# Splitting the two parts of a weight tile in TensorE's queue: high parts first, low parts second

## The chip, the cores and the metric

The kernel runs on one core of a Trainium2 chip. Its metric is the device time in microseconds (us) of one execution of the whole program. Before the change three runs took 1864.05, 1870.47 and 1871.99 us, the median is 1870.47 us. One more execution was recorded by the profiler and took 1869.3 us. In the profile PE is TensorE's matmul, PEld its weight load, DVE VectorE, ACT ScalarE, POOL GpSimd and SP SyncE.

## The reference

One block of a transformer on 256 tokens of width 2048, all in float32:

```python
h = rms_norm(x, norm_mix_g) * (1 + scale_m) + shift_m      # from mod = silu(c) @ ada_w + ada_b
proj = h @ w_in                                            # gMLP and mLSTM inputs
...
x = x + gate_m * (concatenate([y_g, y_m]) @ w_out)
h = rms_norm(x, norm_ffn_g) * (1 + scale_f) + shift_f
q = (h @ w_query).reshape(T, 8, 2, 128)                    # 8 heads, two halves
s1, s2 = q[:, :, 0] @ sub_keys_1.T, q[:, :, 1] @ sub_keys_2.T
...                                                        # top 16 of each, top 16 of the 256 sums
act = gelu(einsum("td,thkd->thk", h, expert_down[idx]))
y = einsum("thk,thkd->td", gates * act, expert_up[idx])
x = x + gate_f * y;  out = rms_norm(x, final_norm_g)
```

There are 16384 experts, each one row of `expert_down` and one of `expert_up`.

## The kernel before

The kernel keeps float32 accuracy with TensorE's fp32r format. A weight tile `raw` (128 x 2048) comes by DMA, ScalarE copies it to fp32r (`H`, the high part, L152) and VectorE subtracts (`L`, the low part, L153), both in halves of 1024 columns; `H` and `L` have three buffers each of one half, `raw` has three. Activations are stored as a high and a low part side by side (`hT[:, k, 0, :]` and `hT[:, k, 1, :]`, 256 tokens each). One step k of a matrix product is H by high, H by low, and L by high.

Two routines issue these steps. `gemm_t` (with `gemm_k`) issues three products of 256 columns into one half of a PSUM bank; it makes the 24 tiles of `w_ct` and the 16 of `w_out`. `gemm_2` (with `gemm_w`) issues one product of H with both parts, 512 columns (L176), and then one of L with 256 columns (L177), and `join` adds the two halves of the bank afterwards. It makes the 16 tiles of the PEER queries (`w_q`) and the 128 tiles of the down projection, in which every expert is evaluated for every token. Each tile has 16 steps. The first two query tiles are an exception: they are made together, half by half, while the normalised activations `hF` are still being written, with `gemm_w` alternating between the two banks.

While the query and down tiles run, a list of background work is issued in pieces, `background(step)` after each tile: top-16 selections, softmax, 32 gate units in four chunks, the storing and masking of the chunks, the last modulation columns (`ada_gf`, DMA and VectorE), and list pieces that sort the used rows. Each entry has an estimated cost, and an entry is issued when the costs so far lie under `BG_RATE * step`. A gate unit makes two one-hot tiles (L703) and three weighted ones (L708) on VectorE in bfloat16, each with two buffers, then 24 products of 128 columns on TensorE (L722), and two copies out of PSUM by ScalarE (L727). A list piece makes four such tiles and 16 products (L890, L891). `tc.issue_after(last_l[0])` puts the background's VectorE work behind the last issued L split.

The framework orders each engine's instructions by a planner: where an instruction was issued and its priority decide, as far as the planner's own estimate of what is ready allows; each engine then executes its queue strictly in that order. The splits of weight tiles are issued with raised priority. When the background list is done (`open_up`), the buffers of the last stage are laid out, and behind the 128 down tiles comes the tail: rows of activations and of `expert_up` are gathered by index, split, and multiplied into eight PSUM banks (L1202).

Of the kernel before, what the change touches and what calls it, by code (L numbers as in the profile page):

```python
# [19 lines left out]
P = 128  # L20
D = 2048
KT = D // P
T = 256
# [9 lines left out]
GP = 8  # L33
# [11 lines left out]
def block_kernel(ctx: ExitStack, tc: tile.TileContext, I: dict, out: bass.AP):  # L45
# [15 lines left out]
    mm = nc.tensor.matmul  # L61
# [77 lines left out]
    last_l = [None]  # L139
# [15 lines left out]
            Ls.append(L)  # L155
        return Hs, Ls

    def gemm_k(o, HL, hT, k, slot, first, last):
        H, L = HL[0][slot // 8], HL[1][slot // 8]
        ks = slice((slot % 8) * P, (slot % 8 + 1) * P)  # L160
        mm(o, H[:, ks], hT[:, k, 0, :], start=first, stop=False)
        mm(o, H[:, ks], hT[:, k, 1, :], start=False, stop=False)  # L162
        mm(o, L[:, ks], hT[:, k, 0, :], start=False, stop=last)

    def gemm_t(src, hT, name, order=tuple(range(KT))):
        HL = load_split(src)
        ps = bank(name)
        for n, k in enumerate(order):
            gemm_k(ps[:, :T], HL, hT, k, n, n == 0, n == KT - 1)
        return ps  # L170

    def gemm_w(o, HL, hT, k, first, last):

        H, L = HL[0][k // 8], HL[1][k // 8]
        ks = slice((k % 8) * P, (k % 8 + 1) * P)
        mm(o, H[:, ks], hT[:, k, :, :].rearrange("p a t -> p (a t)"), start=first, stop=last, skip_group_check=True)  # L176
        mm(o[:, :T], L[:, ks], hT[:, k, 0, :], start=False, stop=last, skip_group_check=True)  # L177

    def gemm_2(src, hT, name):
        HL = load_split(src)  # L180
        ps = bank(name)
        for k in range(KT):
            gemm_w(ps, HL, hT, k, k == 0, k == KT - 1)
        return ps

    def join(dst, ps):
# [505 lines left out]
    def gate_unit(u):  # L692
# [20 lines left out]
            gp_cm.append(gp_cm[0].__enter__())  # L713
        if q == 0:
            gch[ch] = gp_cm[1].tile([P, P, TCH], F32, tag="gch", name="gch")
        gc = gch[ch]
        for half in range(2):
            ps = bank("ps_G")
            for n in range(4):
# [149 lines left out]
        ls.update(cb=cb, v1=v1, pcol=pcol, ps=bank("ps_idx"))  # L869

    def list_c(c):
        lh, cb, v1, pcol, ps = (ls[n] for n in ("lh", "cb", "v1", "pcol", "ps"))
        t0 = 8 * c

        def bc(ap):
            return ap[:, t0 : t0 + 8].rearrange("p (a b) -> p a b", b=2).unsqueeze(2).to_broadcast([P, 4, P, 2])

        io = iota2.unsqueeze(1).to_broadcast([P, 4, P, 2])
        lo = ex.tile([P, 4, P, 2], BF16, tag="oh0", bufs=2, name="llo")
        V.tensor_tensor(lo, io, bc(lh[:, 0, :]), op=ALU.is_equal)  # L880
        hi = ex.tile([P, 4, P, 2], BF16, tag="oh1", bufs=2, name="lhi")
        V.tensor_tensor(hi, cb.unsqueeze(1).to_broadcast([P, 4, P, 2]), bc(lh[:, 1, :]), op=ALU.is_equal)
        hv = ex.tile([P, 4, P, 2], BF16, tag="oa0", bufs=2, name="lhv")
        V.tensor_tensor(hv, hi, bc(v1), op=ALU.mult)
        lv = ex.tile([P, 4, P, 2], BF16, tag="oa1", bufs=2, name="llv")
        V.tensor_scalar(lv, lo, pcol[:, 0:1], None, op0=ALU.mult)
        for t in range(8):
            a, b = t // 2, t % 2
            first, last = c == 0 and t == 0, c == 15 and t == 7
            mm(ps[:, 0:P], lo[:, a, :, b], hv[:, a, :, b], start=first, stop=last, skip_group_check=True)  # L890
            mm(ps[:, P : 2 * P], lv[:, a, :, b], hi[:, a, :, b], start=False, stop=last, skip_group_check=True)  # L891
# [42 lines left out]

    def units(ch):
        n = TCH // 8
        return [(0, 3.1, lambda u=u: gate_unit(u)) for u in range(n * ch, n * ch + n)]

    def leave(ch):
        return [(0, 1.2, lambda p=p: (gate_store(ch, p), gate_mask(ch, p, GP))) for p in range(GP)]  # L940
# [19 lines left out]
    for h in range(8):  # L960
# [8 lines left out]
    bg += [(0, 4.5, lambda p=p: gate_mask(3, p, 2)) for p in range(2)]  # L969
    bg += [(0, 8.0, list_a)]  # L970
    bg += mixed(
        [(0, 5.0, list_b)] + [(0, 2.5, lambda c=c: list_c(c)) for c in range(16)],
        [(0, 0.0, lambda p=p: gate_store(3, p)) for p in range(GP)],
    )
    bg += [(0, 2.0, list_d)]
    bgi = 0
    spent = 0.0

    def background(step):
        nonlocal bgi, spent  # L980
        while bgi < len(bg) and bg[bgi][0] < step and spent < BG_RATE * step:
            spent += bg[bgi][1]
            with tc.issue_after(last_l[0]):
                bg[bgi][2]()
            bgi += 1

    step = 0
    for h in range(8):
        if h == 0:
            pq = [bank("ps_q0"), bank("ps_q1")]  # L990
            w2 = [load_raw(I["w_q"][i]) for i in range(2)]
            for half in range(2):
                parts = []
                for i in range(2):
                    H = wp.tile([P, 1024], F32R, tag="H", bufs=3, name="H")
                    L = wp.tile([P, 1024], F32R, tag="L", bufs=3, name="L")
                    r = w2[i][:, half * 1024 : (half + 1) * 1024]
                    nc.scalar.activation(H, r, AF.Copy)
                    nc.vector.tensor_tensor(L, r, H.bitcast(F32), op=ALU.subtract)
                    parts.append(([H, H], [L, L]))  # L1000
                for k in range(8 * half, 8 * half + 8):
                    for i in range(2):
                        gemm_w(pq[i], parts[i], hF, k, k == 0, k == KT - 1)
            qq = [q_copy(p) for p in pq]
            step += 1
        else:
# [46 lines left out]
    for j in range(NE):  # L1053
# [9 lines left out]
            nc.scalar.dma_start(agV[:, j : j + 1, 0:T], actg[:, j % AB : j % AB + 1, :])  # L1063
        background(step)
        step += 1
        if bgi == len(bg) and not R:
            print("background done at", j)
            done_at = j
            open_up()
# [276 lines left out]
```

## Time and profile before

| what | value |
|---|---|
| median of three runs | 1870.47 us |
| profiled execution, its time | 1869.3 us |
| its span, first to last instruction | 1867.5 us |
| PE busy | 1780.6 us, 95% |
| VectorE busy | 1476.7 us, 79% |
| ScalarE busy | 914.3 us, 49% |
| mean granted clock of TensorE | 0.977 of full speed |

Stages in the span: modulation, first norm and gate projections to about 160 us; `w_ct` and `w_out` tiles to 501 us; second norm and the query tiles to 622 us; down tiles to 1430 us, the gate units among them from 667 to 1227 us and the list pieces from 1278 to 1384 us; then the tail.

An instruction's duration on PE contains the time in which it fills and drains the array, and several overlap; the distance between two starts is the pace. A row of the timeline gives the start in us from the span's start, the duration in us, engine, line, operation, and what is written and read; an entry in brackets is the idle time before it and what ended it.

### The profile page before, as it was taken

The page shows a single profiled execution, that of the slowest core. Times are in us where ns is not written, and L with a number is a line of the kernel's source. Part 1 is how long each engine was busy: PE and PEld are TensorE (multiplying, and loading weights), DVE is VectorE, ACT ScalarE, POOL GpSimd, SP SyncE. Part 2 cuts the span into 40 slices and gives each one's busy share as a digit, 9 for nine tenths or more (in the row PEclk, how much of TensorE's full clock was granted, in tenths as well). Part 3 has the DMA queues.
Part 4 walks back from the last instruction along what each step waited for, and adds up shares of the span by engine and source line. Part 5 has one row for each costly group of instructions (what it writes and reads, how often), then busy time and mean ns, then how long its engine had stood idle before and what let it go on. Part 6 is the DMA issues. An engine that isn't in the chain of part 4 may idle for free. (4 is left out here: it accounts for less than half of the span.)

```text
span 1867.5 us, 27509 instructions
## 1 busy us (share of the span) xinstructions
PE 1780.6 (95%) x10516; PEld 1501.2 (80%) x10516; DVE 1476.7 (79%) x2379; ACT 914.3 (49%) x1285; POOL 258.3 (14%) x231
## 2 busy tenths in 40 slices
PE   5889999999889999999999999999998999999995
PEld 3336999999878878888888878888887888888884
DVE  6887889888769977996997789778765777777776
ACT  1116554544454455455456434654444555555654
POOL 0000000000000000000000000000002555656660
PEclk8989999999999999999999999999999999999998
DMA  9997888778555546955964998487565899989992
GB/s 375 363 353 277 341 318 318 265 268 330 204 192 187 176 165 195 279 201 169 288 220 163 324 336 303 171 241 237 183 224 199 324 401 328 324 315 335 327 330 90
DMA packets 153310, 496.94 MB, mean 266 GB/s; under 512 B 76008, under 2 KB 92264, under 8 KB 102096
## 3 DMA queue, kind: packets, MB, share of 16 engines
q1 hardware_dynamic: 47560, 327.55, 47.4%
q0 software_dynamic: 22400, 129.92, 19.2%
q10 hardware_dynamic: 83208, 37.56, 7.4%
q8 instruction: 91, 1.49, 0.3%
q14 instruction: 51, 0.42, 0.1%
HBM read 457.49 MB, written 37.50 MB: 265 GB/s over the span
## 5 line engine op out<-in xcount | busy, mean ns | idle before, releaser
L176 PE MATMUL ps_z<-hT_f,H 128*128 128x512 f32 x2048 | 733.8, 402 | 3.0 <-ACT H L152 3.0
L152 ACT ACTIVATE H<-raw 128x1024 fp32r<-128x1024 f32 x390 | 412.0, 1059 | 478.9 <-PE ps_z L176 235.4
L153 DVE TENSOR_TENSOR L<-raw,H 128x1024 fp32r<-128x1024 f32 x390 | 473.1, 1220 | 186.0 <-ACT H L152 181.1
L177 PE MATMUL ps_z<-hT_f,L 128*128 128x256 f32 x2048 | 577.4, 282 | 2.1 <-DVE L L153 2.0
L176 PEld LDWEIGHTS ps_z<-hT_f,H 128*128 128x128 f32 x2048 | 386.9, 189 | 97.6 <-ACT H L152 4.0
L177 PEld LDWEIGHTS ps_z<-hT_f,L 128*128 128x128 f32 x2048 | 389.2, 190 | 3.6 <-DVE L L153 3.5
L1180 DVE TENSOR_TENSOR uL<-uraw,uH 128x1024 fp32r<-128x1024 f32 x194 | 228.6, 1219 | 103.0 <-ACT uH L1163 103.0
L1163 ACT ACTIVATE uH<-uraw 128x1024 fp32r<-128x1024 f32 x194 | 195.0, 1053 | 174.4 <-PE ps_y L1202 152.0
L113 DVE SCALAR_TENSOR_TENSOR acc<-araw,sT,acc 128x512 f32<-128x512 f32 (+1 forms) x240 | 243.9, 1017 | 7.7 <-DMA araw<-ada_gf 1.6
L1202 PE MATMUL ps_y<-uH,uWH 128*128 128x512 f32 x584 | 230.9, 395 | 3.4 <-issue 3.4
L1202 PE MATMUL ps_y<-uL,uWH 128*128 128x512 f32 x584 | 228.6, 391 | 0.0
L1202 PE MATMUL ps_y<-uH,uWL 128*128 128x512 f32 x584 | 228.5, 391 | 0.0
L1021 POOL DMA_INDIRECT agr<-agD,idxG x99 | 138.5, 1399 | 123.8 <-DVE uWL L1182 98.8
L1021 POOL DMA_INDIRECT uraw<-up,idxU x99 | 107.9, 1090 | 173.8 <-DVE idxU L901 107.5
L1202 PEld LDWEIGHTS ps_y<-uH,uWH 128*128 128x128 f32 x584 | 110.7, 190 | 26.0 <-issue 3.8
L1202 PEld LDWEIGHTS ps_y<-uH,uWL 128*128 128x128 f32 x584 | 110.3, 189 | 23.1
L1202 PEld LDWEIGHTS ps_y<-uL,uWH 128*128 128x128 f32 x584 | 110.5, 189 | 22.1
L227 PE MATMUL ps_v<-w,xhat 128*128 128x512 f32 x192 | 96.1, 655 | 9.8 <-ACT xhat L198 9.8
L176 PE MATMUL ps_q<-hT_f,H 128*128 128x512 f32 x256 | 94.7, 410 | 6.9 <-DVE hT_f L576 6.9
L227 PEld LDWEIGHTS ps_v<-w,xhat 128*128 128x128 f32 x192 | 38.7, 209 | 57.9 <-issue 47.4
L1059 ACT ACTIVATE actg<-actg 128x256 f32<-128x256 f32 x128 | 53.0, 415 | 57.6 <-DVE actg L188 57.6
L162 PE MATMUL ps_wo<-yT,H 128*128 128x256 f32 x256 | 73.8, 288 | 1.8 <-DVE yT L530 1.8
(377 smaller groups left out, 2558.4 us busy)
## 6 DMA issues: line engine op xcount, KB each, us to landing
raw<-down SPq DMA_DIRECT2D x128, 1024.0 KB, 4.9
araw<-ada_sm SPq DMA_DIRECT2D x32, 1024.0 KB, 7.7
raw<-w_ct SPq DMA_DIRECT2D x32, 1024.0 KB, 7.2
araw<-ada_sf SPq DMA_DIRECT2D x32, 1024.0 KB, 7.0
araw<-ada_gm SPq DMA_DIRECT2D x16, 1024.0 KB, 5.4
raw<-w_out SPq DMA_DIRECT2D x16, 1024.0 KB, 7.0
raw<-w_q SPq DMA_DIRECT2D x16, 1024.0 KB, 4.8
araw<-ada_gf SPq DMA_DIRECT2D x16, 1024.0 KB, 6.0
```

What stands on the lines that cost most here:

```text
L113: nc.vector.scalar_tensor_tensor(acc, w, sc_, acc, op0=ALU.mult, op1=ALU.add)
L152: nc.scalar.activation(H, r, AF.Copy)
L153: last_l[0] = nc.vector.tensor_tensor(L, r, H.bitcast(F32), op=ALU.subtract).ins
L162: mm(o, H[:, ks], hT[:, k, 1, :], start=False, stop=False)
L176: mm(o, H[:, ks], hT[:, k, :, :].rearrange("p a t -> p (a t)"), start=first, stop=last, skip_group_check=True)
L177: mm(o[:, :T], L[:, ks], hT[:, k, 0, :], start=False, stop=last, skip_group_check=True)
L227: mm(bk, h, w[:, off + c * 512 : off + (c + 1) * 512], start=first, stop=last)
L1021: return nc.gpsimd.indirect_dma_start(out_, None, tab, bass.IndirectOffsetOnAxis(ap=idx[:, b : b + 1], axis=0))
L1059: nc.scalar.activation(z, z, AF.Gelu)
L1163: a.activation(H[:, c], raw[:, c], AF.Copy).then_inc(s_h, 1)
L1180: v.tensor_tensor(L[:, c], raw[:, c], H[:, c].bitcast(F32), op=ALU.subtract).then_inc(s_l, 1)
L1202: m_ = t.matmul(ps_y[tt][c], x, y[:, cs], start=False, stop=False, skip_group_check=True)
```

## The change

In `gemm_t` and `gemm_2` all products of a half tile with `H` are issued first, for its eight steps, and then the eight with `L`. `gemm_w` becomes `half_w`, which takes one bank or two, so that the first query pair has the same order (two H products per step for eight steps, then sixteen L products). The number of products and what they compute stay the same.

The products of gate units and list pieces are put into functions of their own. An entry of the background list that carries a fourth element hands its products back, and they are issued at the beginning of the next `background` call, behind the next tile; an entry without it first issues whatever is still held back. The ScalarE copies out of PSUM move with the products. The estimated costs stay.

```diff
--- before.py
+++ after.py
@@ -155,32 +155,39 @@
             Ls.append(L)
         return Hs, Ls
 
-    def gemm_k(o, HL, hT, k, slot, first, last):
-        H, L = HL[0][slot // 8], HL[1][slot // 8]
-        ks = slice((slot % 8) * P, (slot % 8 + 1) * P)
-        mm(o, H[:, ks], hT[:, k, 0, :], start=first, stop=False)
-        mm(o, H[:, ks], hT[:, k, 1, :], start=False, stop=False)
-        mm(o, L[:, ks], hT[:, k, 0, :], start=False, stop=last)
-
     def gemm_t(src, hT, name, order=tuple(range(KT))):
-        HL = load_split(src)
+        H, L = load_split(src)
         ps = bank(name)
-        for n, k in enumerate(order):
-            gemm_k(ps[:, :T], HL, hT, k, n, n == 0, n == KT - 1)
+        o = ps[:, :T]
+        for q in range(2):
+            for n in range(8 * q, 8 * q + 8):
+                ks = slice((n % 8) * P, (n % 8 + 1) * P)
+                for x in range(2):
+                    mm(o, H[q][:, ks], hT[:, order[n], x, :], start=(n == 0 and x == 0), stop=False)
+            for n in range(8 * q, 8 * q + 8):
+                ks = slice((n % 8) * P, (n % 8 + 1) * P)
+                mm(o, L[q][:, ks], hT[:, order[n], 0, :], start=False, stop=(n == KT - 1))
         return ps
 
-    def gemm_w(o, HL, hT, k, first, last):
-
-        H, L = HL[0][k // 8], HL[1][k // 8]
-        ks = slice((k % 8) * P, (k % 8 + 1) * P)
-        mm(o, H[:, ks], hT[:, k, :, :].rearrange("p a t -> p (a t)"), start=first, stop=last, skip_group_check=True)
-        mm(o[:, :T], L[:, ks], hT[:, k, 0, :], start=False, stop=last, skip_group_check=True)
+    def half_w(banks, Hs, Ls, hT, q):
+
+        for k in range(8 * q, 8 * q + 8):
+            ks = slice((k % 8) * P, (k % 8 + 1) * P)
+            for o, H in zip(banks, Hs):
+                mm(
+                    o, H[:, ks], hT[:, k, :, :].rearrange("p a t -> p (a t)"),
+                    start=(k == 0), stop=(k == KT - 1), skip_group_check=True,
+                )
+        for k in range(8 * q, 8 * q + 8):
+            ks = slice((k % 8) * P, (k % 8 + 1) * P)
+            for o, L in zip(banks, Ls):
+                mm(o[:, :T], L[:, ks], hT[:, k, 0, :], start=False, stop=(k == KT - 1), skip_group_check=True)
 
     def gemm_2(src, hT, name):
-        HL = load_split(src)
+        H, L = load_split(src)
         ps = bank(name)
-        for k in range(KT):
-            gemm_w(ps, HL, hT, k, k == 0, k == KT - 1)
+        for q in range(2):
+            half_w([ps], [H[q]], [L[q]], hT, q)
         return ps
 
     def join(dst, ps):
@@ -713,7 +720,9 @@
             gp_cm.append(gp_cm[0].__enter__())
         if q == 0:
             gch[ch] = gp_cm[1].tile([P, P, TCH], F32, tag="gch", name="gch")
-        gc = gch[ch]
+        return lambda: gate_products(gch[ch], q, oh, oa)
+
+    def gate_products(gc, q, oh, oa):
         for half in range(2):
             ps = bank("ps_G")
             for n in range(4):
@@ -869,7 +878,7 @@
         ls.update(cb=cb, v1=v1, pcol=pcol, ps=bank("ps_idx"))
 
     def list_c(c):
-        lh, cb, v1, pcol, ps = (ls[n] for n in ("lh", "cb", "v1", "pcol", "ps"))
+        lh, cb, v1, pcol = (ls[n] for n in ("lh", "cb", "v1", "pcol"))
         t0 = 8 * c
 
         def bc(ap):
@@ -884,6 +893,10 @@
         V.tensor_tensor(hv, hi, bc(v1), op=ALU.mult)
         lv = ex.tile([P, 4, P, 2], BF16, tag="oa1", bufs=2, name="llv")
         V.tensor_scalar(lv, lo, pcol[:, 0:1], None, op0=ALU.mult)
+        return lambda: list_products(c, lo, lv, hi, hv)
+
+    def list_products(c, lo, lv, hi, hv):
+        ps = ls["ps"]
         for t in range(8):
             a, b = t // 2, t % 2
             first, last = c == 0 and t == 0, c == 15 and t == 7
@@ -934,7 +947,7 @@
 
     def units(ch):
         n = TCH // 8
-        return [(0, 3.1, lambda u=u: gate_unit(u)) for u in range(n * ch, n * ch + n)]
+        return [(0, 3.1, lambda u=u: gate_unit(u), True) for u in range(n * ch, n * ch + n)]
 
     def leave(ch):
         return [(0, 1.2, lambda p=p: (gate_store(ch, p), gate_mask(ch, p, GP))) for p in range(GP)]
@@ -969,19 +982,32 @@
     bg += [(0, 4.5, lambda p=p: gate_mask(3, p, 2)) for p in range(2)]
     bg += [(0, 8.0, list_a)]
     bg += mixed(
-        [(0, 5.0, list_b)] + [(0, 2.5, lambda c=c: list_c(c)) for c in range(16)],
-        [(0, 0.0, lambda p=p: gate_store(3, p)) for p in range(GP)],
+        [(0, 5.0, list_b)] + [(0, 2.5, lambda c=c: list_c(c), True) for c in range(16)],
+        [(0, 0.0, lambda p=p: gate_store(3, p), True) for p in range(GP)],
     )
     bg += [(0, 2.0, list_d)]
     bgi = 0
     spent = 0.0
 
+    rest = []
+
+    def flush():
+        while rest:
+            rest.pop(0)()
+
     def background(step):
         nonlocal bgi, spent
+        with tc.issue_after(last_l[0]):
+            flush()
         while bgi < len(bg) and bg[bgi][0] < step and spent < BG_RATE * step:
             spent += bg[bgi][1]
             with tc.issue_after(last_l[0]):
-                bg[bgi][2]()
+                late = bg[bgi][3:]
+                if not late:
+                    flush()
+                r = bg[bgi][2]()
+                if late and r:
+                    rest.append(r)
             bgi += 1
 
     step = 0
@@ -990,17 +1016,16 @@
             pq = [bank("ps_q0"), bank("ps_q1")]
             w2 = [load_raw(I["w_q"][i]) for i in range(2)]
             for half in range(2):
-                parts = []
+                Hs, Ls = [], []
                 for i in range(2):
                     H = wp.tile([P, 1024], F32R, tag="H", bufs=3, name="H")
                     L = wp.tile([P, 1024], F32R, tag="L", bufs=3, name="L")
                     r = w2[i][:, half * 1024 : (half + 1) * 1024]
                     nc.scalar.activation(H, r, AF.Copy)
                     nc.vector.tensor_tensor(L, r, H.bitcast(F32), op=ALU.subtract)
-                    parts.append(([H, H], [L, L]))
-                for k in range(8 * half, 8 * half + 8):
-                    for i in range(2):
-                        gemm_w(pq[i], parts[i], hF, k, k == 0, k == KT - 1)
+                    Hs.append(H)
+                    Ls.append(L)
+                half_w(pq, Hs, Ls, hF, half)
             qq = [q_copy(p) for p in pq]
             step += 1
         else:
@@ -1063,7 +1088,7 @@
             nc.scalar.dma_start(agV[:, j : j + 1, 0:T], actg[:, j % AB : j % AB + 1, :])
         background(step)
         step += 1
-        if bgi == len(bg) and not R:
+        if bgi == len(bg) and not rest and not R:
             print("background done at", j)
             done_at = j
             open_up()
```

## Rows read from the trace of the kernel before

**Rows 1.** Page, busy time of PE (share of the span, instructions), whole run
```profile
PE 1780.6 (95%) x10516; PEld 1501.2 (80%) x10516; DVE 1476.7 (79%) x2379; ACT 914.3 (49%) x1285; POOL 258.3 (14%) x231
```

**Rows 2.** Page, granted TensorE clock in 40 slices, tenths of full speed
```profile
PEclk8989999999999999999999999999999999999998
```

**Rows 3.** Page, costliest groups: total busy us, mean ns | idle before
```profile
L176 PE MATMUL ps_z<-hT_f,H 128*128 128x512 f32 x2048 | 733.8, 402 | 3.0 <-ACT H L152 3.0
L177 PE MATMUL ps_z<-hT_f,L 128*128 128x256 f32 x2048 | 577.4, 282 | 2.1 <-DVE L L153 2.0
```

**Rows 4.** Window, L176 alone: length, PE busy (count), PEld, clock, DMA share, GB/s
```profile
732.20:822.50 90.30, 90.30 (x256) 48.00 (x256) 1.00 0.82 255
```

**Rows 5.** Timeline of PE: start us, duration us; eight high products, alternating
```profile
639.61 0.39 PE L176 MATMUL ps_z<-hT_f,H 128*128 128x512 f32 x1
...
642.04 0.39 PE L176 MATMUL ps_z<-hT_f,H 128*128 128x512 f32 x1
```

**Rows 6.** Timeline of PE, tail, 512-column products, eleven steps apart
```profile
1499.75 0.39 PE L1202 MATMUL ps_y<-uH,uWL 128*128 128x512 f32 x1
...
1502.24 0.39 PE L1202 MATMUL ps_y<-uL,uWH 128*128 128x512 f32 x1
```

**Rows 7.** Timeline of PE, 256-column products, 34 steps apart; group of their weight loads
```profile
249.84 0.28 PE L161 MATMUL ps_qk<-hT_m,H 128*128 128x256 f32 x1
...
253.91 0.28 PE L162 MATMUL ps_qk<-hT_m,H 128*128 128x256 f32 x1
...
L163 PEld LDWEIGHTS ps_qk<-hT_m,L 128*128 128x128 f32 x256 | 49.0, 192 | 0.8 <-issue 0.4 <-DVE L L153 0.2
```

**Rows 8.** Timeline of PE, first gate unit; window: PE, PEld, DVE, ACT, POOL, clock
```profile
662.36 0.27 PE L675 MATMUL ps_gt<-ident,gate 128*128 128x128 f32 x1
666.95 0.39 PE L722 MATMUL ps_G<-oa,oh 128*128 128x128 bf16 x2 [4.32 <-DVE oa L708]
...
668.88 2.36 PE L722 MATMUL ps_G<-oa,oh 128*128 128x128 bf16 x20
671.00 0.78 PE L176 MATMUL ps_z<-hT_f,H 128*128 128x512 f32 x1
...
666.05:672.85 6.80, 5.90 (x33) 5.12 (x34) 2.71 (x8) 2.10 (x2) 0.00 (x0) 0.50 0.00 0
```

**Rows 9.** Timeline of VectorE (DVE) around the first gate unit
```profile
660.61 1.22 DVE L153 TENSOR_TENSOR L<-raw,H 128x1024 fp32r<-128x1024 f32 x1 [1.16 <-ACT H L152]
...
668.13 0.69 DVE L708 TENSOR_TENSOR oa<-oh,g 128x1024 bf16<-128x1024 bf16 x1
```

**Rows 10.** Waits of PE by releaser: us in total, times, longest us
```profile
PE ps_G L722 <- DVE oa L708: 4.3, 1, 4.3
...
PE ps_z L176 <- ACT H L152: 3.0, 2, 2.4
...
PE ps_z L177 <- DVE L L153: 2.0, 3, 0.8
```

**Rows 11.** Window as in group 8; timeline of ScalarE (ACT) near 1088
```profile
1032.60:1088.00 55.40, 52.06 (x292) 44.04 (x289) 41.38 (x41) 21.47 (x32) 0.00 (x0) 1.00 1.01 338
...
1088.14 1.06 ACT L152 ACTIVATE H<-raw 128x1024 fp32r<-128x1024 f32 x1 [8.03 <-issue]
```

**Rows 12.** Timeline of PE, end of the first query pair
```profile
523.54 0.50 PE L176 MATMUL ps_q<-hT_f,H 128*128 128x512 f32 x1 [0.83 <-DVE hT_f L576]
...
526.36 0.28 PE L177 MATMUL ps_q<-hT_f,L 128*128 128x256 f32 x1
```

**Rows 13.** Timeline of PE, VectorE, a later gate unit; window as in group 8
```profile
689.61 1.55 PE L722 MATMUL ps_G<-oa,oh 128*128 128x128 bf16 x24
690.97 0.48 PE L176 MATMUL ps_z<-hT_f,H 128*128 128x512 f32 x1
...
689.10 1.28 DVE L703 TENSOR_TENSOR oh<-iota,it 128x1024 bf16<-128x1024 bf16 x2
...
683.88:698.06 14.18, 14.18 (x116) 12.45 (x114) 11.40 (x16) 9.29 (x13) 0.00 (x0) 1.00 0.47 157
```

## The prediction

> **What bounds the kernel now.** I began with the busy times: PE works 95% of the span, so a gain has to come from PE itself: from the pace of its products, its idle time, or its clock [rows 1]. The clock line of the 40 slices shows full speed nearly everywhere behind the start, with short dips [rows 2]. The groups by cost then name the place: two lines of one routine, the product with a high weight part (L176, 512 columns) and the one with a low part (L177, 256 columns), 2048 each for the down projection alone [rows 3]. A mean duration there (402 and 282 ns) says little, because products overlap in PE; what counts is the distance from start to start, which the timeline gives.
>
> A stretch of 90.3 us with nothing but such pairs holds 256 of them: 0.3527 us a pair [rows 4]. Earlier, ahead of the first gate products, seven pairs take 642.04 - 639.61 = 2.43 us, 0.347 each [rows 5]. Now the two kinds alone. The tail issues 512-column products one behind the other, eleven steps in 1502.24 - 1499.75 = 2.49 us: 0.2264 us each [rows 6]. The convolution tiles issue 256-column products one behind the other, 34 steps in 253.91 - 249.84 = 4.07 us: 0.1197 us each, though a weight load lasts 192 ns by its own row: consecutive loads overlap [rows 7]. So 0.2264 + 0.1197 = 0.3461 us for two products that cost 0.3527 us when they alternate. PE loses 6.6 ns per pair in taking turns.
>
> The other losses are stops. At the first gate unit PE finishes the transposes at 662.4 and then waits for the one-hot tiles of VectorE; the unit's products end at 671.0, and the granted clock was 0.50 from 666.05 to 672.85 [rows 8]. The waits by releaser name this stop (4.3 us), and small ones for H (3.0) and for L (2.0) in the down projection [rows 10].
>
> **The change, part by part.**
>
> *High products first, then low ones, in tiles with 512-column products.* No instruction is added or dropped: 16 tiles of the query projection and 128 of the down projection, 16 pairs each. From the first gate unit on there are 121 down tiles (seven lie ahead of it in the timeline); 121 x 16 x 6.6 ns = 12.8 us [rows 4, 6, 7]. The seven ahead of it gain nothing, since 0.347 us is already the sum of the two runs [rows 5]. For the 16 query tiles, which lie between, I take half: 16 x 16 x 3.3 ns = 0.8 us, an estimate with ends 0 and 1.7. Each half tile keeps one turn from high to low and one back; if each such pair of turns costs the whole 6.6 ns, 288 halves return 1.9 us, if none 0; I take 1.0. Sum: 12.6 us. One stretch can't keep its share: from 1032.6 to 1088.0 the DMA share is 1.01 while PE is busy 52.06 of 55.4 us [rows 11]; there the transfers set the pace, and the 1.0 us that nine or ten tiles would gain is waited away again. What is left: 11.6 us.
>
> A rule of the Trainium skill speaks against this term. Its page "TensorE: Matmul & The Clock Gate", section "Wait — 56ns, not 53.3ns?", gives a warm start-to-start distance of N / 2.4 GHz plus about 2.5 ns for every matmul; by it 512 and 256 columns are 215.8 + 109.2 = 325 ns in any order, and the reordering is worth nothing. This trace does not agree: its runs show 226.4 and 119.7 ns, its alternation 352.7.
>
> *The same order in tiles with 256-column products* (w_ct and w_out, 40 tiles): all three products of a step have 256 columns and already follow each other at 0.1197 us [rows 7]. Taken at nothing. Bounds: the rows are rounded to 10 ns, over 34 steps 0.3 ns a product, and 40 tiles of 48 products make 0.6 us to either side of it.
>
> *What the order does to buffers.* H of a half tile is free after its high products, 8 x 0.12 = 1.0 us earlier; L of a half is wanted 8 x 0.2264 = 1.8 us later than H instead of at once. The 2.0 us of waits for L [rows 10] should go; what is late next is H, so I take 1 us of gain, bounds 0 and 2. The H wait of 2.4 us near 1086 stays: ScalarE came to H at 1088.14 after 8.03 us in which it was stuck behind its own DMA issues, no buffer was missing [rows 11].
>
> *The first query pair.* It runs while hF is still being made. The last piece of hF comes at 523.54, and PE's two tiles end with the low product that starts at 526.36, eight pairs or 2.8 us [rows 12]. After the change eight high products (1.8 us) and all sixteen low ones of the half (1.9 us) stand behind that piece: 3.7 us, 0.9 us more. It is exposed, since the scores wait for both tiles. Bounds: 0 (the fourth H buffer comes free earlier, and with it the splits behind) to 2.
>
> *Gate and list products one step behind.* 32 gate units with 24 products and 16 list pieces with 16; their number stays. Before, the first unit's products stand right behind the transposes that its own VectorE work needs. Between 662.4 and 671.0 PE does 24 gate products (1.36 us by the regular unit, 689.61 to 690.97) and two pairs (0.7 us), so 6.5 us are lost; up to 672.85 another 1.85 us run at 0.50, costing 0.9 us: 7.4 us [rows 8, 13]. With a tile of 5.6 us put between, PE has work: VectorE finished the L of that tile's first half at 660.61 + 1.22 = 661.8 [rows 9]. The last one-hot product of VectorE is ready at 668.13 + 0.69 = 668.8, or 1.2 us later with one more split in front, while PE comes to the gate products at about 668.0: 1 us of wait stays. Gain 6.4 us, bounds 0 (rival C) and 7.4. The other units lose nothing now: they start in step with the last product of a tile [rows 13]. The due times of the background list stay, since the plan's costs are unchanged, so the tail opens behind the same tile.
>
> **Sum.** 11.6 + 1.0 + 6.4 - 0.9 = 18.1 us. Against the profiled execution, 1869.3 us: 1851.2. Its median of three stands 1.2 us higher, at 1870.5, and there the forecast is 1852 us.
>
> **Rivals.**
>
> B, *the pace does not follow the order*: the 6.6 ns is a state into which PE falls at the first gate product, as 0.347 before it suggests [rows 4, 5], and it stays in grouped runs. Against: the tail and the tiles of 256 columns pace evenly, the former behind that point [rows 6, 7]. Then only 6.4 + 1.0 - 0.9 = 6.5 us come: 1864 us. The rule of the Trainium skill's page above leads to this time too, and its chance is in B's.
>
> C, *the first unit's stop stays*. The instruction order comes from a planner with its own durations; it can put the unit's products ahead of the tile again, as it split them around two pairs before. For: PE did not take the tile that was ready at 661.8. Against: the tile now has the earlier place. Then 11.7 us: 1859 us.
>
> D, *slower: VectorE waits for the one-hot buffers*. There are two of each. Before, unit u+1 writes its first one-hot at 689.10, when the products of unit u-1 are long done; after, those products stand where 689.61 to 690.97 is now, and the write waits 1.87 us, with everything queued behind it on VectorE: the other one-hots, the join, the L splits for which PE waits. VectorE has 14.18 - 11.40 = 2.8 us idle for two units, 1.4 us each [rows 13]. If the idle takes none of it, 32 x 1.87 = 60 us are added: 1912 us; it decides from 18.1 / 32 = 0.57 us of PE time per unit. Against: L splits are ordered ahead by priority, L is wanted later than before, and the idle time covers most.
>
> **How the numbers follow.** Forecast (A) 0.74, B 0.11, C 0.08, D 0.07. What a measurement of this kernel can tell from no change is 0.5%, 9.4 us, so faster means under 1861.1 us. A is faster but for 0.02; C mostly (0.06 of 0.08); B lies within (0.10); D is slower but for 0.01. Faster 0.79, same 0.15, slower 0.06. The range: the lower end takes each term at its better bound: 12.8 + 1.7 of pace with turns free and nothing returned, 2.3 more for the rounding of the rows (0.9 ns a step of 512 columns and 0.3 of 256, over 121 x 16 pairs), 7.4, 2.0, 0.6 and no loss at the query pair, 26.8 us, so 1844. The upper end reaches to B: 1865.
>
> **What would show it.** A down tile between gate units should take 16 x 0.3461 = 5.54 us instead of 5.64; starts inside a run 227 and 120 ns apart. No wait of PE for VectorE's oa tiles over 2 us, and no half clock near 666. The first scores a little later behind hF. VectorE waiting for PE's gate products would show D at work. I would be wrong if the pair stays at 353 ns when grouped, or if PE waits for L inside the gate stage.

## The result, and the profile after

The changed kernel takes 1851.3 us (median of five runs, 1848.7 to 1854.1) against 1870.5: a ratio of 0.990 (95%: 0.988 to 0.992). The forecast was 1852. Its profiled execution has a span of 1851.7 us, where the one before had 1867.5: the two profiles differ by 15.8 us, the medians by 19.1. The total came out as forecast; the terms behind it did so only in part, and two errors of opposite sign cancelled.

The page of the kernel after, the busy line, two of its costliest groups and the clock line, answers to [rows 1 to 3]:

```profile
PE 1768.6 (96%) x10516; PEld 1501.8 (81%) x10516; DVE 1478.4 (80%) x2379; ACT 918.6 (50%) x1285; POOL 258.4 (14%) x231
...
PEclk8999999999989999999999999999999999999998
...
L177 PE MATMUL ps_z<-hT_f,H 128*128 128x512 f32 x2048 | 520.3, 396 | 2.9 <-ACT H L152 2.9
...
L184 PE MATMUL ps_z<-hT_f,L 128*128 128x256 f32 x2048 | 285.3, 282 | 0.0
```

The instruction counts are those of before. The low products (now L184) have no idle time ahead of them any more; before, they had 2.1 us. The fall of a group's busy sum (733.8 to 520.3 us) is no gain: overlapping products of one group are counted once, and in a run they stand beside their own kind. The pace has to be read from starts. PE's timeline in a stretch without gate products, start and duration in us; the last row is the first product 13 tiles behind the first row:

```profile
745.86 2.00 PE L177 MATMUL ps_z<-hT_f,H 128*128 128x512 f32 x8
747.70 1.11 PE L184 MATMUL ps_z<-hT_f,L 128*128 128x256 f32 x8
748.65 2.00 PE L177 MATMUL ps_z<-hT_f,H 128*128 128x512 f32 x8
750.49 1.11 PE L184 MATMUL ps_z<-hT_f,L 128*128 128x256 f32 x8
751.44 0.40 PE L177 MATMUL ps_z<-hT_f,H 128*128 128x512 f32 x1
...
818.48 0.40 PE L177 MATMUL ps_z<-hT_f,H 128*128 128x512 f32 x1
```

And the first products of two tiles of before, 13 tiles apart:

```profile
743.49 0.40 PE L176 MATMUL ps_z<-hT_f,H 128*128 128x512 f32 x1
...
816.99 0.40 PE L176 MATMUL ps_z<-hT_f,H 128*128 128x512 f32 x1
```

A tile takes 751.44 - 745.86 = 5.58 us; 13 tiles in a row take 72.62, 5.587 each, where 13 of before take 73.50, 5.654 each. The same engine in the kernel after, at the first gate unit [rows 8]:

```profile
666.94 0.27 PE L682 MATMUL ps_gt<-ident,gate 128*128 128x128 f32 x1
666.97 2.09 PE L177 MATMUL ps_z<-hT_f,H 128*128 128x512 f32 x8
668.90 1.11 PE L184 MATMUL ps_z<-hT_f,L 128*128 128x256 f32 x8
...
672.64 0.29 PE L731 MATMUL ps_G<-oa,oh 128*128 128x128 bf16 x2
672.74 1.86 PE L177 MATMUL ps_z<-hT_f,H 128*128 128x512 f32 x7
```

And the same window as there, then one 4.2 us later, by which this execution reaches its first down tile later; the columns are those of [rows 8]:

```profile
666.05:672.85 6.80, 6.80 (x45) 6.08 (x45) 5.74 (x12) 3.69 (x5) 0.00 (x0) 1.00 0.54 167
670.26:677.06 6.80, 6.80 (x51) 5.66 (x51) 6.48 (x12) 2.39 (x3) 0.00 (x0) 1.00 0.47 157
```

A whole tile now stands between the transposes and the unit's first product. PE is busy through both windows and its clock stays at 1.00, where it was 0.50. The waits of PE by releaser (us in total, times, longest) have no line for ps_G and none for L in the down projection [rows 10]:

```profile
PE ps_z L177 <- ACT H L152: 2.9, 1, 2.9
PE ps_y L1227 <- issue: 2.6, 1, 2.6
```

To see where the time came from, I cut each profile at the starts of the same products (us; q is the first query product, z0 the first down product, z67 that of down tile 67, counted from 0, gf the first product of the second half of the last modulation columns, z121 that of tile 121; the tail's entry lies between the last down product and the first tail product, the tail runs from there to the last one; q-end is everything from q on):

```
                   start-q  q-z0  z0-z67  z67-gf  gf-z121  tail entry  tail   q-end
before               508.4 113.8   421.8   107.5    238.8        11.8  403.9 1359.1
before, 2nd          511.0 115.4   416.8   105.5    238.8        12.5  402.6 1352.7
before, 3rd          510.8 115.2   421.5   105.3    238.8        11.7  402.6 1357.0
after                511.9 114.4   412.1   101.7    236.8        11.0  402.6 1339.8
after, 2nd           510.9 114.3   412.1   101.2    236.8        11.0  402.6 1339.2
order only           512.5 114.4   418.8   105.8    237.4        12.6  401.0 1351.0
order only, 2nd      511.8 114.4   418.8   105.5    237.4        11.0  402.6 1350.7
late only            511.0 115.4   413.5   106.3    240.2        12.5  402.6 1352.2
late only, 2nd       510.1 114.0   415.2   104.7    240.2        12.5  401.0 1349.2
runs of 16           511.0 114.2   411.9   109.9    236.4        15.8  403.8 1353.0
runs of 4            510.5 115.5   412.8   104.9    240.0        12.9  402.6 1350.0
stores on GpSimd     512.3 114.4   411.9   104.1    238.2        11.0  402.6 1343.4
only 1st unit late   511.9 114.5   412.1   104.0    237.4        12.4  402.6 1344.0
narrow order old     512.1 114.3   412.1   101.4    236.8        11.0  402.6 1339.4
```

Between before and after, the stretch up to tile 67 gives back most. The next largest piece, at the last modulation columns, is one to which the forecast gave nothing. The column start-q differs between executions of one program: with 511.0 and 510.8 us in the two repeats of before, the 508.4 of its first profile is chance.

### The profile page after: what moved, and what is told of

Read it like the earlier page. It is cut to its first block, busy times and chain, and to the rows that moved or that the text cites. A ratio compares the mean times of both kernels' runs of the same rounds, so it can differ in the third digit from the quotient of the medians.

```text
span 1851.7 us, 27519 instructions
## 1 busy us (share of the span) xinstructions
PE 1768.6 (96%) x10516; PEld 1501.8 (81%) x10516; DVE 1478.4 (80%) x2379; ACT 918.6 (50%) x1285; POOL 258.4 (14%) x231
## 5 line engine op out<-in xcount | busy, mean ns | idle before, releaser
L177 PE MATMUL ps_z<-hT_f,H 128*128 128x512 f32 x2048 | 520.3, 396 | 2.9 <-ACT H L152 2.9
L177 PEld LDWEIGHTS ps_z<-hT_f,H 128*128 128x128 f32 x2048 | 368.6, 189 | 71.0 <-ACT H L152 3.1
L184 PEld LDWEIGHTS ps_z<-hT_f,L 128*128 128x128 f32 x2048 | 279.3, 190 | 20.4
L184 PE MATMUL ps_z<-hT_f,L 128*128 128x256 f32 x2048 | 285.3, 282 | 0.0
L177 PE MATMUL ps_q<-hT_f,H 128*128 128x512 f32 x256 | 69.6, 414 | 8.2 <-DVE hT_f L583 8.1
L736 ACT ACTIVATE gch<-ps_G 128x512 f32<-128x512 f32 x64 | 65.7, 1127 | 9.8 <-PE ps_G L731 9.8
```

What stands on the lines that cost most here:

```text
L184: mm(o[:, :T], L[:, ks], hT[:, k, 0, :], start=False, stop=(k == KT - 1), skip_group_check=True)
L736: nc.scalar.activation(gc[:, :, o0 : o0 + 4].rearrange("p i t -> p t i"), ps.rearrange("p (t i) -> p t i", t=4), AF.Copy)
```

## The experiments

**The two parts alone.** Order without the delay (products issued with their unit again):

```diff
-                late = bg[bgi][3:]
+                late = ()
...
-                if late and r:
-                    rest.append(r)
+                if callable(r):
+                    r()
```

> The new product order alone: gate and list products are issued with their unit again. Theory T (the two parts are separate: order sets the pace, holding back removes the stop at the first gate unit): a down tile between stops takes 5.59 us from start to start as in the changed kernel, 0.06 us under the 5.65 of before, 120 tiles make 7 to 8 us; the stop of some 7 us behind the transposes is back; with 0 to 5 us from the stretch in which the last modulation columns are loaded, 1858 to 1864 us. Rival R1 (the pace follows from what stands around the gate products, not from the order): tiles of 5.65 us, 1867 to 1871 us. Rival R2 (the two parts work only together, since the planner orders everything anew): neither the pace nor the stop comes out as in these sums, and the time lies outside both ranges.

And the delay without the order (in gemm_t and half_w each low product goes back behind the high product of its step):

```diff
-            for o, H in zip(banks, Hs):
+            for o, H, L in zip(banks, Hs, Ls):
...
-        for k in range(8 * q, 8 * q + 8):
...
-            for o, L in zip(banks, Ls):
```

> The held-back gate and list products alone: every product routine alternates high and low as before. Theory T: tiles of 5.65 us behind the first gate unit and 5.55 ahead of it, as before; the stop at the first gate unit is gone (7.3 us by the two traces, tile starts compared); with 0 to 5 us from the stretch of the last modulation columns, if the held-back products are what shortened it, 1858 to 1863.5 us. Rival R1 (the gate products set the pace): tiles of 5.59 us or less, 1851 to 1856 us.

Measured: order only 1864.7 us, 0.9986 (0.9976 to 0.9995); late only 1865.5 us, 0.9985 (0.9977 to 0.9994). Three to four us each, beside 19 for the whole, and both a little above the ranges expected (1864 and 1863.5 us at most). Each does what it should at its place: order only has tiles of 5.587 us, and late only crosses the first gate unit without a stop. PE's waits in the down projection and the gate stage, order only and then late only:

```profile
PE ps_z L177 <- ACT H L152: 6.1, 3, 3.6
PE ps_G L731 <- DVE oa L715: 4.2, 1, 4.2
```

```profile
PE ps_z L175 <- ACT H L152: 5.6, 1, 5.6
PE ps_z L179 <- DVE L L153: 2.0, 2, 1.5
```

The order alone keeps the stop at ps_G (4.2 us); late alone has no such line. Both show more waiting for H than before (3.0) or after (2.9).

**Is the sum real?** Unchanged repeats of the changed kernel and of both parts:

> The changed kernel once more, beside its two parts on one chip. The parts alone gave 4.0 and 3.3 us, their sum 7.3, the whole 19.1. Theory T (pace and stop add up as in the traces; on top the plan of the whole has less waiting in the stretch of the last modulation columns, from tile 64 to the last column product 120.1 us against 124 to 128 in the four other versions): 1849 to 1853 us again. Rival N (the 19 us hold some luck of that chip or of those runs): 1857 to 1862 us, which is what the parts add up to.

> The product order alone, a second time, for a second profile. Theory T: counted from the first query product the execution is some 8 us shorter than before, made of 2.9 us up to tile 64 and the rest behind it; the early stage, whose instructions are the same, differs by some us from execution to execution. If T is right the same stages differ again by the same amounts (within 1 us), apart from the early stage and the entry of the tail. Rival N (all differences of a few us are chance): the stages come out otherwise, up to 5 us off.

> The held-back products alone, a second time, for a second profile. Theory T: up to tile 64 some 8 us shorter than before again, the stop of 1.9 us for L near 1239 (list making) is there again, and the H stop of some 6 us in the stretch of the last modulation columns too: both belong to this version's plan. Rival N: these two stops are chance, and the second profile lacks at least one of them.

1849.6 us for the whole (0.9899, 0.9883 to 0.9914), 1865.1 (0.9982) and 1865.0 (0.9979) for the parts. The stages of order only come out again to within 0.4 us, apart from start-q and a shift of 1.6 us between the tail and its entry; those of late only to within 1.7. So the parts don't add: -3.5 and -3.7 make -7.2, the whole is -19.1. The table tells in part where, against the mean of the three profiles of before. Up to tile 67 the whole has -7.9, the parts -1.2 and -5.7: they nearly add. From there to gf the whole has -4.7, the parts -0.5 and -0.6; from gf to tile 121 -2.0, against -1.4 and +1.4. So the surplus that the profiles show lies behind tile 67, where other transfers and splits meet PE. Over the whole way from q to the end it is about 6 us (-16.8, against -5.4 and -5.6), half of the 12 by medians; each profile is one execution, and where the rest lies they don't show.

**What a turn costs.** If the tile's loss sits in the turns between 512 and 256 columns, its length must follow their number. One run of 16 high and 16 low products, then runs of four:

```diff
-        for q in range(2):
-            half_w([ps], [H[q]], [L[q]], hT, q)
+        for k in range(KT):
...
+            mm(ps, H[k // 8][:, ks], ...)
+        for k in range(KT):
...
+            mm(ps[:, :T], L[k // 8][:, ks], ...)
```

> The changed kernel with runs of sixteen in the query and down tiles (first query pair as changed): all sixteen high products of a tile, then all sixteen low ones. Theory T (what is left of the gain is lost at turns: behind a turn from low to high the first five high products start 233, 236, 228, 233 and 231 ns apart instead of 227, and the first low one after high comes 113 instead of 120: 26 ns for each half tile): half the turns, 5.565 us per tile instead of 5.59, 142 tiles make 3.5 us, 1848 us, if the planner finds room for the low parts, which are wanted 1.8 us later. Rival S (the loss is one of every product in this stage, whatever the order): 5.59 us per tile and 1851 us. Rival U (a buffer of the low part comes free later, VectorE falls behind and PE waits for L): PE waits for L show up, over 1853 us.

```diff
+        for k0 in range(8 * q, 8 * q + 8, run):    # run = 4 in gemm_2
-        for k in range(8 * q, 8 * q + 8):
+            for k in range(k0, k0 + run):
```

> The changed kernel with runs of four in the query and down tiles: four high products, four low ones, four times a tile (first query pair as changed). Theory T (a loss per turn): the first four high products behind a turn cost 233, 236, 228 and 233 ns, the four low ones 113 + 3 x 120: 1403 ns per run, 5.61 us per tile, 1.5 to 3 us slower than the changed kernel, 1853 to 1855 us. Rival S (a loss of every product, whatever the order): 5.59 us per tile, 1851 us. Rival V (short runs lock into one of the two even paces of the alternating order, 5.55 or 5.65): 1846 or 1859 us.

Timelines of PE, runs of 16 and then of four:

```profile
740.49 3.82 PE L191 MATMUL ps_z<-hT_f,H 128*128 128x512 f32 x16
744.15 2.08 PE L197 MATMUL ps_z<-hT_f,L 128*128 128x256 f32 x16
746.06 3.82 PE L191 MATMUL ps_z<-hT_f,H 128*128 128x512 f32 x16
```

```profile
740.30 1.09 PE L178 MATMUL ps_z<-hT_f,H 128*128 128x512 f32 x4
741.23 0.63 PE L185 MATMUL ps_z<-hT_f,L 128*128 128x256 f32 x4
741.70 1.09 PE L178 MATMUL ps_z<-hT_f,H 128*128 128x512 f32 x4
```

Over 13 tiles: 5.567 us with one pair of turns in a tile, 5.587 with two, 5.613 with four. Turns cost time, in that order, and the tiles are those expected (5.565 and 5.61). The totals missed their expectations all the same: 1862.3 us (0.997, 0.9954 to 0.9986) and 1862.8 us (0.9973, 0.9964 to 0.9982); the executions with runs of 16 spread from 1853.7 to 1869.2 us. In the profile, one of 1866.1 us, the kernel with the best tile loses 8.5 us to the changed one between tile 67 and gf and 4.8 at the tail's entry. Its waits of PE name both places:

```profile
PE ps_z L191 <- ACT H L152: 7.9, 3, 3.6
PE ps_y L1234 <- issue: 7.3, 1, 7.3
```

**Is alternation slow in every execution?** The kernel before, profiled twice more:

> The kernel before once more, for a second profile. Theory T (the early stage differs by chance: in the profile of before the first query product started at 508.4 us, in the eight others at 510.1 to 512.5): it starts at 510 to 512 here, and the stretch from tile 64 to the last column product takes less than the 126.0 us of before, since the whole agrees with the median. Rival N (the early stage is shorter in the kernel before for a reason): 508 to 509 us again.

> The kernel before a third time, as the run ahead of it and for the same two numbers. Theory T: the first query product at 510 to 512 us in at least one of the two, and the stop at the first gate unit (6.6 us from the last transpose to the end of its products but for two pairs) in both. Rival N: 508 to 509 us in both.

No. In a window of 73.5 us, PE never idle and its clock full, L176 alone (length, PE busy with count, PEld with count, clock, DMA share, GB/s), in the second profile of before and then in the third:

```profile
743.50:817.00 73.50, 73.50 (x213) 39.82 (x212) 1.00 0.85 265
```

```profile
747.00:820.50 73.50, 73.50 (x209) 39.16 (x209) 1.00 0.82 259
```

Four more pairs in the same time. Start to start, the second profile takes 2.78 us for eight pairs, in these two rows of its timeline:

```profile
752.08 0.39 PE L176 MATMUL ps_z<-hT_f,H 128*128 128x512 f32 x1
...
754.86 0.39 PE L176 MATMUL ps_z<-hT_f,H 128*128 128x512 f32 x1
```

That is 347 ns a pair, as in [rows 5], and not the 353 of [rows 4]. The same program has two paces: of its plain down tiles, those with no other product between, 39 run at 5.55 us and 15 at 5.65 in the second profile, 7 and 45 in the first, 1 and 54 in the third. 39 tiles that are 0.1 us shorter make most of the difference between 416.8 and 421.8 or 421.5 us in the table. Grouped tiles have one pace in both profiles of after: 54 plain ones at 5.59, none at 5.55, one at 5.65.

**Who sets the time at the last modulation columns?** There ScalarE issues the stores of the gate chunks from its own queue. Moved to GpSimd's:

```diff
-        nc.scalar.dma_start(agV[:, a:e, ...], gch[ch][:, a:e, :])
+        nc.gpsimd.dma_start(agV[:, a:e, ...], gch[ch][:, a:e, :])
```

> The changed kernel with the stores of the gate chunks issued from GpSimd instead of ScalarE, 32 DMAs. Theory Q (in the stretch of the last modulation columns PE waits because ScalarE stands behind its own DMA issues, up to 9.7 us at once, while H is due): ScalarE's waits at issue fall from 36 us to under 10, PE's stop of 2.9 us and the half clock behind it go, 3 to 5 us less: 1847 us. Rival M (the transfers themselves set the time there, DMA share 0.97 to 1.04): ScalarE waits less, but H then waits for raw tiles; 1850 to 1853 us. Rival G (GpSimd's descriptors for 2048 short rows a store take longer than the hardware queue's): the stores finish late, the masks and the next chunk wait, over 1856 us.

1856.6 us, 0.9928 (0.9915 to 0.9942): 7 us worse than the changed kernel's 1849.6 beside it. In the kernel after, ScalarE's timeline shows a store in its queue for 10.93 us, and the H behind it late by 9.73:

```profile
1057.24 10.93 ACTq L743 DMA_DIRECT2D agD<-gch  x1
1058.19 0.37 ACT L194 ACTIVATE actg<-ps_z 128x256 f32<-128x256 f32 x1
1068.29 1.06 ACT L152 ACTIVATE H<-raw 128x1024 fp32r<-128x1024 f32 x1 [9.73 <-issue]
```

Waits of ScalarE in the kernel after, then of ScalarE and of PE with the stores moved:

```profile
ACT H L152 <- issue: 36.4, 20, 9.7
...
ACT H L152 <- DMA raw<-down: 4.9, 5, 2.1
```

```profile
ACT H L152 <- DMA raw<-down: 17.2, 7, 5.0
ACT H L152 <- issue: 17.2, 12, 1.5
```

```profile
PE ps_z L177 <- ACT H L152: 2.9, 1, 2.9
```

The long issue waits are gone (1.5 us at most, where it was 9.7); instead H waits longer for the weights themselves, and PE's stop is 2.9 us as before. The edit changed one thing more, the stores' own time. The list of DMA issues, for the kernel after and then with the stores moved, gives the median from issue to landing in its last column:

```profile
agD<-gch ACTq DMA_DIRECT2D x28, 512.0 KB, 8.5
```

```profile
agD<-gch POOLq DMA_DIRECT2D x28, 512.0 KB, 15.1
```

That is the rival with slow stores, and the time lies in its range (over 1856 us). So this run shows that the issue waits alone don't set PE's stop, but not what a queue as fast as ScalarE's, and free, would bring. The window of the kernel after around the stop shows how full the transfers are (columns of [rows 11]):

```profile
1038.40:1089.70 51.30, 48.42 (x263) 40.78 (x261) 42.64 (x43) 22.05 (x35) 0.00 (x0) 0.97 1.04 357
```

The transfers fill the stretch: DMA share 1.04 at 357 GB/s, beside 1.01 at 338 in [rows 11]. That the stuck queue and the late tile both come from this one limit is likely, but not shown.

**Is holding back one unit enough?** Only the first gate unit stays a step behind; the other 31, the list pieces and the stores of the last chunk go back (the lines for the two latter are left out here):

```diff
-        return [(0, 3.1, lambda u=u: gate_unit(u), True) for u in ...]
+        return [(0, 3.1, lambda u=u: gate_unit(u), u == 0) for u in ...]
...
```

> The changed kernel with only the first of the 32 gate units held back; all other gate and list products are issued with their unit. Theory T (holding back is worth something at the first unit alone; other units' products were never waited for): the stop at the first unit stays away, up to tile 64 the time is that of the changed kernel, and the whole lies at 1849 to 1856 us, the width for what the plan makes of the later stretches. Rival W (the held-back products of the other units carry the rest, by what they free in ScalarE's and VectorE's queues): the pace of the tiles between gate units gets worse or stops appear there, 1857 to 1863 us.

1857.6 us, 0.9947 (0.9932 to 0.9962), above the 1849 to 1856 expected of it. Up to tile 67 it equals the changed kernel to the tenth (412.1 us): between gate units the delay of the others gives nothing. What is missing, 6 us by medians and 4.5 by profiles, lies behind tile 67: 104.0 instead of 101.7 or 101.2, 237.4 instead of 236.8, 12.4 instead of 11.0.

**The narrow tiles.** High, high, low again in gemm_t alone:

```diff
-            for n in range(8 * q, 8 * q + 8):
-                ks = slice((n % 8) * P, (n % 8 + 1) * P)
                 mm(o, L[q][:, ks], hT[:, order[n], 0, :], ...)
```

> The changed kernel with the old order (high, high, low at each step) in the tiles with 256-column products, w_ct and w_out. Theory T (all products there have 256 columns and one pace): from the first v product of w_v1 to the last of w_out the time is 344.3 to 344.8 us in all profiles so far and stays there; 1849 to 1853 us. Rival X (the order there matters through the H buffers, which come free earlier): that stage is over 346 us, 1852 to 1856 us.

1852.8 us, 0.9925 (0.9908 to 0.9942). These tiles stand ahead of q, from the first product of `w_v1` to the last of `w_out`: 344.7 us here, 344.5 in both profiles of after, 344.7 in the three of before. Behind q the stretches are those of after to within 0.4 us. That edit is worth nothing that can be told from chance.

## Why the prediction held, and where it did not

**The first gate unit: right.** Forecast 6.4 us. Tiles 5 to 7 took 25.81 us before and 17.20 after, 8.6 less; the unit's 24 products (1.36 us) now stand later. Net 7.3 us; against the other two profiles of before, with 24.94 and 25.01 us, it is 6.4. The 1 us of wait that I left at the new place is not there: the planner spread the unit's products over the next tile, two, two and twenty, as VectorE's tiles came. Rival C is out. That the delay does it, and the order does not, the two parts alone show; that one unit's delay suffices, the run with only the first unit late shows.

**The pace: the mechanism right, the size too large.** The term that was mis-sized is the charge for turns: 1.0 us for 288 half tiles, with a bound of 1.9. The rows give 8 + 8 products from 745.86 to 748.65, 2.793 us in the mean of the 13 tiles. Single starts in that stretch show where the time goes: the first five high products behind a low run are 233, 236, 228, 232 and 231 ns apart, the later ones 226.7; the first low start is 113 ns ahead of the second, the second 119 ahead of the third, the rest 120.0. Eight steps of each kind at the steady 226.7 + 120.0 make 2.773 us, so a pair of turns costs 20 ns net, and runs of 16 and of 8, one pair apart, say the same: 5.567 and 5.587 us a tile. Over 288 half tiles that is 5.8 us. I had held that a pair of turns costs at most what a pair loses in alternation, 6.6 ns; it costs three times that. (The 6.6 itself stands: the two readings behind it, 0.3527 and 0.3461 us, are both 0.6 ns low, since whole tiles of before give 353.3 ns a pair.) So a plain tile takes 5.587 us instead of the 5.54 forecast; the gain is 5.654 - 5.587 = 0.067 us, and 121 of them make 8 us where 12.6 were expected with the query tiles. Where gate units stand it is less: from tile 9 to tile 67 order only takes 357.0 us and the first and third profiles of before 360.1, which is 0.053 us a tile, 6 us for 121.

**Rival B: half right.** It said that 353 ns is a state of PE and not a cost of order. There are two paces of alternation, and an execution can keep the fast one far behind the first gate products, as the second profile of before does until tile 54. But the grouped order has neither: it runs evenly, 1.2% faster than the slow pace and 0.7% slower than the fast one. The forecast took the slow pace of one profile for that of the kernel. For the seven tiles ahead of the first gate unit it said "gain nothing"; against that profile they lose 0.04 us each (5.59 for 5.55), against the third, with 5.65 there, they gain.

**The last modulation columns: missed.** The forecast gave it zero, 1.0 us of pace returned. From tile 67 to gf the changed kernel takes 4 to 6 us less, about 1 of them pace (18 tiles), and this only in the three profiles in which the wide tiles' order, every delayed product and the stores' queue are those of the changed kernel (101.2 to 101.7 us; 104.0 and more in all others, runs of 16 and of four among them). That ScalarE was "stuck behind its own DMA issues, no buffer was missing" is not the whole cause, as far as the moved stores show: with the long issue waits gone, PE stops as long as before. In the kernel after, the gate-chunk stores stand one tile later and the first load of the modulation columns stands ahead of them. That this order saves the transfers their time was not tried by itself, and it does not seem to be enough: with runs of four the first load is ahead of the stores too, and the stretch takes 104.9 us. What makes it cheap stays open. "The other units lose nothing now" holds between the units, as forecast, but not here: their delay, with that of the list pieces and of the last chunk's stores, is worth about 5 us at the far end of the list.

**The rest.** H and L waits: L's 2.0 us are gone and H's hardly changed, within the bounds. First query pair: its last low run starts at 529.10 with 16 products, 0.95 us later behind hF's last piece than before [rows 12], as worked out, but the first score product stands 6.77 us behind that piece where it was 6.50, so 0.3 us of it reach the scores; q to z0 is 114.4 us, between the 113.8 and 115.4 of before, so no cost can be told. Narrow tiles: nothing, as said. Rival D: VectorE has no wait for gate products anywhere, though the next one-hot begins only while a unit's products run (from 685.40). VectorE's load did not change: over two units it is busy for 11.40 of 14.08 us, where it was 11.40 of 14.18 [rows 13]. Timeline of VectorE, then the window with the columns of [rows 8]:

```profile
685.70 0.68 DVE L710 TENSOR_TENSOR oh<-iota,it 128x1024 bf16<-128x1024 bf16 x1
```

```profile
686.76:700.84 14.08, 14.08 (x116) 12.62 (x114) 11.40 (x15) 9.37 (x13) 0.00 (x0) 1.00 0.45 161
```

The two large errors, some 5 us too much of pace and 5 us too little from the modulation columns on, nearly cancel. The forecast of 18.1 us was met by 19.1, and that the total agrees so well is luck.

**Open.** Why the tail's entry takes 11.0 us here and 12.4 to 15.8 there (PE's wait there is named "issue", 2.6 us in one and 7.3 in another; two executions of order only have 12.6 and 11.0, so part of it is not the plan), and what in the combination makes the last modulation columns cheap. No variant beat the changed kernel: runs of 16 have the better tile and the worse total.

## What to carry to other kernels

Price an order change on PE by starts over whole tiles, not by adding two pure paces: the turns themselves cost, and only a stretch that contains them shows it. Read the pace of before from more than one profile, since alternating shapes can run at two. Where parts of a change move the plan, measure the whole: parts that give 4 us each gave 19 together, and as far as the profiles show the surplus it lies behind tile 67, some 370 us after the first gate unit, in stretches that the forecast had put at nothing.

## What the hardware showed that I had not expected

Products of 512 and 256 columns in alternation took 347 or 353 ns a pair in one and the same program, at a granted clock of 1.00 and with PE never idle; the pace changes within an execution and from one execution to the next. In runs of eight and of 16, after a change from 256 to 512 columns, the next five starts are up to 10 ns slower than the steady 226.7, and a pair of turns costs 20 ns. With the DMA share at 1.04, one store issue held ScalarE's queue for 10.93 us. The page "TensorE: Matmul & The Clock Gate" of the Trainium skill, section "Wait — 56ns, not 53.3ns?", gives N / 2.4 GHz plus about 2.5 ns from one back-to-back product to the next on the full clock; by it a tile's 16 pairs would take 5.2 us in any order, an estimate. The measurements disagree: the fastest tiles take 5.55, and the order moves them by up to 0.1.
